# Layer normalisation with its gain and shift applied behind the transposition, in a two-layer decoder trunk on one core

## The chip, the cores and the metric

The kernel runs on one core of one Trainium2 chip. Its time is the device time of one execution in microseconds (us); three runs of the kernel before were timed, and their median is the reference point. Beside them one execution was recorded by the hardware profiler. Five engines work in parallel, each with its own queue of instructions: TensorE (PE, matrix products and transpositions, with its weight loads PEld), VectorE (DVE), ScalarE (ACT), GpSimd (POOL) and SyncE (SP), which here issues nearly all transfers (DMA).

## What is computed

Two layers, each a token mixer and a squared-ReLU feed-forward, in float32, with 1024 positions, a model width of 1024 and a feed-forward width of 4096:

```python
for i in range(2):
    y = dilated_attention_mixer(x, ...) if i == 0 else hgrn2_mixer(x, ...)
    x = layer_norm(alpha * x + y, ln_mix_g[i], ln_mix_b[i])
    y = squared_relu_mlp(x, ffn_w_up[i], ffn_w_down[i])
    x = layer_norm(alpha * x + y, ln_ffn_g[i], ln_ffn_b[i])
```

`layer_norm` subtracts the mean of a row, divides by its standard deviation, multiplies by a gain g and adds a shift b, each a vector of 1024. So every normalised x has two uses: it is the left operand of the next products, and it is the residual of the next sum. Call the value ahead of g and b the unit value.

## The kernel before, in words

A float32 product is made of three matmuls: each operand is split in a high part (an ACT copy that rounds) and a low part (a DVE subtraction), and high times high, low times high and high times low are summed in PSUM. `split` (L137 ACT, L138 DVE) does it for weights and intermediate values, `put` (L233 ACT, L234 DVE) for transposed activations.

The rows of x are held as eight tiles z[t] of 128 positions by 1024. The stages follow one another on the time axis: attention; its output projection with the first normalisation (`outproj_ln`, L886); layer 0's feed-forward (`ffn`, L1015), up products and then down products; the HGRN mixer (`hgrn`, L1482); its `outproj_ln`; layer 1's `ffn`, which ends in the output.

**Normalisation.** `ln_math` (L193) takes statistics on DVE (L196, L198), forms (z - mean) * g in one DVE operation over 128x1024 (L199), the reciprocal deviation r from ACT and small DVE operations (L201 to L206), then z * r on ACT (L213) and + b on POOL (L214). Gain and shift are rows that hold for all partitions; they are loaded as broadcasts of 128x1024. The result is stored to DRAM for the later residual (x1d, x3d, x5d). The output's normalisation uses the variant with `store`, in halves on DVE.

**Transposition.** The products need x with the width on the partitions. `z_tr` (L216) has PE transpose a tile in eight 128x128 pieces (L223) into two PSUM banks of tag "pt" (there are two such banks). In the feed-forward's end `ln_tr` (L236) puts high and low straight from PSUM (the tiles f0n). Ahead of the up products the class `Fast` (L248) prepares a fast matrix scheme with seven products of halves in place of eight: it needs the quarters 11, 21, 22 and the combinations T1 to T4. For the four tiles of the half that comes first, `add` (L271) keeps raw copies (ACT, L291 and L292); for the other half it forms T1 to T4 from PSUM and the copies, with DVE (L298, L301) and POOL (L299, L303) subtracting, after one ACT copy (L297).

**Where the transpositions stand.** In `outproj_ln` four tiles are transposed between the last projections (L994 on), and four are handed to the up products as `late` work, one item for each step with two empty steps ahead of each (L1009 to L1011). In the up products `in_order` (L107, used at L1373) pins PE, DVE and SP to the written order; ACT and POOL are ordered by the framework's scheduler.

**The down products** work through i = 1, 6, 7, 5, 4, 2, each 16 steps of 12 matmuls, and then i = 3 in three passes of 16 steps (6, 3 and 3 matmuls). The steps' loads (`load_down`, L1181 on) run 8 steps ahead, their splits 2 or 4 steps ahead (L45 to L47). Nothing pins their order: L1392 opens `in_order(())`, so the scheduler orders every engine. After each step `after(n)` (L1303) issues loads of the residual (L1306 at i = 7, L1308 at i = 5) and of gain and shift (L1310), and takes one item of a list `todo`: adding products into the residual (`mix` L1278, `plus` L1281), normalising a tile (`norm_of` L1291) and, in layer 0, storing it (L1296) and transposing it (`tr` L1286). In layer 0 tiles 4 to 7 are normalised during i = 2, transposed in the passes, and tiles 0 to 3 are normalised and transposed between the passes; `hgrn` then begins with products of f0n. It takes a `late` list too, one item after each block (L1608), which layer 0's `ffn` returns empty.

Tiles of 128x1024 come from one pool of 50 slots (L90); scratch of 128x512 comes from pool wp with 3 buffers for each of the tags "p" and "pts", which d3s and dT3 (the split operands of i = 3, L1220 on) and the transpositions share.

Of the kernel before, what the change touches and what calls it, by code (L numbers as in the profile page):

```python
# [16 lines left out]
P = 128  # L17
# [45 lines left out]
def trunk_kernel(  # L63
# [15 lines left out]
    w_down: bass.AP,  # L79
    cos_t: bass.AP,  # L80
# [53 lines left out]
    nc.gpsimd.memset(one, 1.0)  # L134

# [57 lines left out]
    def ln_math(z, gB, bB, store=None):  # L193
# [5 lines left out]
        nc.vector.scalar_tensor_tensor(z, z, mv[:, 0:1], gB, op0=ALU.subtract, op1=ALU.mult)  # L199
        w = small([P, 4], "lnw")  # L200
# [6 lines left out]
        if store is not None:  # L207
            for i in range(2):
                c = slice(i * 512, i * 512 + 512)
                nc.vector.scalar_tensor_tensor(z[:, c], z[:, c], w[:, 3:4], bB[:, c], op0=ALU.mult, op1=ALU.add)  # L210
                nc.sync.dma_start(store[:, c], z[:, c])
            return
        act(z, z, AF.Copy, scale=w[:, 3:4])  # L213
        nc.gpsimd.tensor_add(z, z, bB)  # L214
# [21 lines left out]
    def ln_tr(t, z, xs):  # L236
        x_ = xs[t // 4]
        c = slice((t % 4) * P, (t % 4) * P + P)
        for j, pt in enumerate(z_tr(z)):
            put(x_.hi[2 * j:2 * j + 2], x_.lo[2 * j:2 * j + 2], pt, c)  # L240

    class Fast:  # L248


        def __init__(self, name):
            self.name, self.parts, self.raw, self.seen = name, {}, {}, []
# [18 lines left out]
        def add(self, t, z):  # L271
# [3 lines left out]
            v, g = nc.vector, nc.gpsimd  # L275
# [5 lines left out]
            def put_(n, src, eng=None):  # L281
                put(*self.tiles(n), src, c, eng)

            if half == 0:
                put_("11", p0)
                put_("21", p1)
            else:
                put_("22", p1)
            if first:
                a, b = ("11", "21") if half == 0 else ("12", "22")  # L290
                act(self.keep(a, t), p0, AF.Copy)  # L291
                act(self.keep(b, t), p1, AF.Copy)  # L292
                return
            t1, t2, t3, t4 = (scratch(n) for n in (1, 2, 3, 4))
            if half == 1:
                w12 = scratch(0)
                act(w12, p0, AF.Copy)  # L297
                v.tensor_sub(t3, p1, w12)  # L298
                g.tensor_sub(t1, w12, self.keep("11", t))  # L299
                put_("T3", t3)  # L300
                v.tensor_sub(t2, p1, t1)  # L301
                put_("T1", t1)
                g.tensor_sub(t4, self.keep("21", t), t2)  # L303
            else:
                b22 = self.keep("22", t)
                v.tensor_sub(t1, self.keep("12", t), p0)
                g.tensor_sub(t3, b22, self.keep("12", t))
                g.tensor_sub(t2, b22, t1)
                put_("T1", t1)
                v.tensor_sub(t4, p1, t2)  # L310
# [11 lines left out]
    def attention(pre, hc):  # L322
# [124 lines left out]
        def constants():  # L447
            nc.sync.dma_start(cosT, cos_t)
            nc.sync.dma_start(sinT, sin_t)
            nc.sync.dma_start(mask, masks)  # L450

# [434 lines left out]
    def outproj_ln(pr, oN, fill, resid, gB_ap, bB_ap, keep):  # L886
# [84 lines left out]
        gB = bcast_rows(gB_ap, "gB")  # L971
        bB = bcast_rows(bB_ap, "bB")
        second(NK)
        xn = Fast(name + "f")
# [4 lines left out]
        def fin(t, dms=(0, 1)):  # L979
# [10 lines left out]
            if 1 in dms:  # L990
                ln_math(z[t], gB, bB)
# [23 lines left out]
    def ffn(li, xf, late, res, gB_ap, bB_ap, last, pre=None):  # L1015
# [261 lines left out]

        def mix(t, c, other):  # L1278
# [7 lines left out]
        def tr(t):  # L1286
            if xn[t // 4] is None:
                xn[t // 4] = new_xT(t // 4, f"f{li}n")
            ln_tr(t, z[t], xn)

        def norm_of(t):  # L1291
            if last:
                ln_math(z[t], norm["g"], norm["b"], out[t * P:(t + 1) * P, :])
                return
            ln_math(z[t], norm["g"], norm["b"])
            nc.sync.dma_start(x3d[t * P:(t + 1) * P, :], z[t])  # L1296
# [454 lines left out]
```

## Time and profile before

| | us |
|---|---|
| three runs: median (lowest to highest) | 2857.04 (2854.59 to 2858.03) |
| the profiled execution | 2856.82 |
| its span, first to last instruction | 2854.6 |
| PE busy in the span | 2789.4 |
| DVE busy | 2053.8 |
| ACT busy | 1448.4 |
| POOL busy | 122.6 |

On the span's time axis layer 0's up products begin at about 1107, its down products run from 1432 to 1755 (i = 7 from 1519, i = 5 from 1562, the three passes from 1696), HGRN follows, layer 1's up products begin at about 2215 and its down products at 2538.

A line of a group reads: line of the code, engine, operation, what is written <- what is read, its shape, how many (x), then busy time in all and the mean in ns of one, then the idle time of the engine ahead of them and what ended it. A line of the waits reads: engine, what it was about to do, <- what it waited for: total us, times, longest. A row of the timeline: start, length, engine, line, operation, and in brackets the idle time ahead and its releaser.

### The profile page before, as it was taken

How to read it: one execution, taken by the hardware profiler on the slowest of the kernel's cores; microseconds unless marked ns; L12 is line 12 of the kernel's file. 1: busy time of each engine (PE TensorE's matmuls, PEld its weight loads, DVE VectorE, ACT ScalarE, POOL GpSimd, SP SyncE). 2: the span in 40 equal slices, each digit the busy share in tenths (PEclk: the TensorE clock that was granted, in tenths of full speed). 3: DMA queues.
4: the chain of work that ended last, by engine and by line, in shares of the span. 5: the costliest groups of instructions: out<-in, count | busy, mean ns of one | idle time of the engine just before them, and what ended most of it. 6: DMA issues, size and time to landing. Idle time of an engine off the chain costs nothing.

```text
span 2854.6 us, 39893 instructions
## 1 busy us (share of the span) xinstructions
PE 2789.4 (98%) x14152; PEld 2235.3 (78%) x14152; DVE 2053.8 (72%) x3830; ACT 1448.4 (51%) x3105; POOL 122.6 (4%) x67
## 2 busy tenths in 40 slices
PE   8999999999999989999999999999999999999998
PEld 6777777777777767888878887778787788878887
DVE  7768777776887767786686875555667787678677
ACT  5555555655555555544454444554553645454433
POOL 0000000000000003000000011111102200000000
PEclk9999999999999999999999999999999999999999
DMA  7766665666667523464584843101131455475654
GB/s 291 249 201 193 190 197 171 215 206 204 198 198 222 154 77 133 156 220 156 173 303 126 275 142 104 38 30 60 51 120 71 159 202 174 155 268 189 223 176 132
DMA packets 204935, 485.25 MB, mean 170 GB/s; under 512 B 29376, under 2 KB 43712, under 8 KB 204736
## 3 DMA queue, kind: packets, MB, share of 16 engines
q1 hardware_dynamic: 204736, 482.72, 51.3%
q8 instruction: 111, 1.82, 0.3%
q14 instruction: 88, 0.72, 0.1%
HBM read 362.82 MB, written 94.24 MB: 160 GB/s over the span
## 4 chain that ended last, share of the span: by engine, by line
PE 90%; DVE 4%; ACT 2%; DMA 1%; issue 1%; POOL 0%; SPq 0%; DVEq 0%; POOLq 0%; ACTq 0%
PE pmm L666 8%; PE pmm L668 8%; PE pmm L667 8%; PE pup L1114 7%; PE pup L1112 7%; PE pup L1113 7%; PE pdy L1264 4%; PE pdy L1260 4%; PE pdy L1263 4%; PE pmm L171 3%; PE s L500 3%; PE pdx L1263 3%; PE pdx L1264 3%; PE pdx L1260 3%; PE pmm L173 3%; PE pmm L172 3%
## 5 line engine op out<-in xcount | busy, mean ns | idle before, releaser
L666 PE MATMUL pmm<-xh,H 128*128 128x512 f32 x1008 | 407.7, 404 | 12.0 <-ACT H L432 8.5
L668 PE MATMUL pmm<-xh,H 128*128 128x512 f32 x1008 | 396.4, 393 | 0.0
L667 PE MATMUL pmm<-xl,H 128*128 128x512 f32 x1008 | 396.1, 393 | 0.0
L666 PEld LDWEIGHTS pmm<-xh,H 128*128 128x128 f32 x1008 | 191.2, 190 | 52.3 <-ACT H L432 8.5
L668 PEld LDWEIGHTS pmm<-xh,H 128*128 128x128 f32 x1008 | 190.4, 189 | 41.9 <-DVE H L440 0.3
L667 PEld LDWEIGHTS pmm<-xl,H 128*128 128x128 f32 x1008 | 191.1, 190 | 36.9
L514 ACT ACTIVATE p<-p,stats 128x128 f32<-128x128 f32 (+1 forms) x384 | 168.3, 441 | 92.6 <-DVE stats L511 92.2
L1263 PE MATMUL pdy<-dT,dS 128*128 128x512 f32 x512 | 199.2, 389 | 0.0
L1260 PE MATMUL pdy<-dT,dS 128*128 128x512 f32 x512 | 199.2, 389 | 0.0
L1264 PE MATMUL pdy<-dT,dS 128*128 128x512 f32 x512 | 199.2, 389 | 0.0
L511 DVE CUSTOM_DVE_ANT_0 p<-s,mask 128x128 f32<-128x128 f32 (+1 forms) x384 | 113.2, 347 | 68.4 <-PE s L500 58.8
L137 ACT ACTIVATE dS<-dr 128x512 fp32r<-128x512 f32 x192 | 119.5, 622 | 73.3 <-PE pdy L1264 36.6
L171 PE MATMUL pmm<-f0nh,wh 128*128 128x512 f32 x384 | 153.1, 399 | 0.0
L173 PE MATMUL pmm<-f0nh,wl 128*128 128x512 f32 x384 | 149.8, 390 | 0.0
L172 PE MATMUL pmm<-f0nl,wh 128*128 128x512 f32 x384 | 149.6, 390 | 0.0
L138 DVE TENSOR_TENSOR dS<-dr,dS 128x512 fp32r<-128x512 f32 x192 | 135.1, 703 | 16.5 <-ACT dS L137 16.5
L214 POOL TENSOR_TENSOR z<-z,bB 128x1024 f32<-128x1024 f32 x24 | 58.5, 2442 | 1687.8 <-ACT z L213 1678.3
L527 ACT ACTIVATE pts<-ppt 128x256 f32<-128x256 f32 (+1 forms) x192 | 85.3, 474 | 62.7 <-PE ppt L524 60.5
L137 ACT ACTIVATE dT<-hold 128x512 fp32r<-128x512 f32 x128 | 80.0, 625 | 69.5 <-DVE hold L1239 28.8
L1073 ACT ACTIVATE H<-wc 128x512 fp32r<-128x512 f32 x128 | 77.2, 625 | 74.6 <-DVE wc L1066 43.9
L1263 PEld LDWEIGHTS pdy<-dT,dS 128*128 128x128 f32 x512 | 96.1, 188 | 20.0
L1264 PEld LDWEIGHTS pdy<-dT,dS 128*128 128x128 f32 x512 | 96.1, 188 | 20.0
(395 smaller groups left out, 6927.9 us busy)
## 6 DMA issues: line engine op xcount, KB each, us to landing
xh<-xtd SPq DMA_DIRECT2D x110, 512.0 KB
xl<-xtd SPq DMA_DIRECT2D x110, 512.0 KB
dr<-hd SPq DMA_DIRECT2D x192, 256.0 KB
dr<-in_w_down_dram SPq DMA_DIRECT2D x128, 256.0 KB
rot<-e SPq DMA_DIRECT2D x192, 128.0 KB
wa<-in_w_up_dram SPq DMA_DIRECT2D x48, 512.0 KB
wb<-in_w_attn_dram SPq DMA_DIRECT2D x36, 512.0 KB
wa<-in_w_attn_dram SPq DMA_DIRECT2D x33, 512.0 KB
```

Source lines behind the costliest of these rows:

```text
L171: nc.tensor.matmul(o, wh[:, k], xs.h(k), start=k == 0, stop=False)
L172: nc.tensor.matmul(o, wh[:, k], xs.l(k), start=False, stop=False)
L173: nc.tensor.matmul(o, wl[:, k], xs.h(k), start=False, stop=k == NK - 1)
L666: nc.tensor.matmul(o, wh, hi[k // 2][:, c], start=begin and k == 0, stop=False, skip_group_check=True)
L667: nc.tensor.matmul(o, wh, lo[k // 2][:, c], start=False, stop=False, skip_group_check=True)
L668: nc.tensor.matmul(o, wl, hi[k // 2][:, c], start=False, stop=end and k == 3, skip_group_check=True)
L1112: nc.tensor.matmul(o, wh, xf.h(b, k), start=begin and k == 0, stop=False, skip_group_check=True)
L1113: nc.tensor.matmul(o, wh, xf.l(b, k), start=False, stop=False, skip_group_check=True)
L1114: nc.tensor.matmul(o, wl, xf.h(b, k), start=False, stop=end and k == 3, skip_group_check=True)
L1260: nc.tensor.matmul(o[q], h, T_[:, L], start=begin, stop=False, skip_group_check=True)
L1263: nc.tensor.matmul(o[q], h, T_[:, R], start=False, stop=False, skip_group_check=True)
L1264: nc.tensor.matmul(o[q], l, T_[:, L], start=False, stop=end, skip_group_check=True)
```

## The change

The three inner normalisations (both mixers', layer 0's feed-forward) leave the unit value in z: ACT computes z * r - mean * r in one pass (`ln_unit`), and L199 and POOL's L214 are gone for them. Gain and shift come in a new small input `lncol`, one value for each partition, normalisation and block of 128 columns, loaded once. After the transposition a new helper `gained` reads a PSUM bank in four pieces of 128x128 with ACT, times the gain and plus the shift as operands per partition, into SBUF; high and low parts and the combinations T1 to T4 are then taken from that SBUF tile. In `Fast` the kept copies are now `gained` tiles, and what POOL subtracted DVE subtracts.

The residual is now read back as a unit value. In the down products of both layers each residual tile is multiplied by the gain and added to the shift on DVE (`gain`, `bias`), one operation a step from the `todo` list, with the two broadcasts rg and rb loaded at i = 7, and the residual's loads are issued at step 4 of i = 7 (before: 8) and step 2 of i = 5 (before: 8). Layer 0's output x3d still holds the full value: `final` multiplies and adds on DVE and stores, as items of the `late` list for `hgrn`. The output's normalisation is as before, in `ln_last`. `outproj_ln` no longer loads gain and shift. All matmuls and transpositions remain.

```diff
-    def ln_math(z, gB, bB, store=None):
+    def ln_scale(z):
...
-        nc.vector.scalar_tensor_tensor(z, z, mv[:, 0:1], gB, op0=ALU.subtract, op1=ALU.mult)
...
-        act(z, z, AF.Copy, scale=w[:, 3:4])
-        nc.gpsimd.tensor_add(z, z, bB)
+    def ln_unit(z):
+        mv = ln_scale(z)
+        w = ln_rsqrt(mv)
+        nc.vector.tensor_scalar(w[:, 4:5], mv[:, 0:1], w[:, 3:4], -1.0, op0=ALU.mult, op1=ALU.mult)
+        act(z, z, AF.Identity, scale=w[:, 3:4], bias=w[:, 4:5])
...
+    def gained(pt, j, col, dst):
+        for i in range(4):
+            k = j * 4 + i
+            c = slice(i * P, i * P + P)
+            act(dst[:, c], pt[:, c], AF.Identity, scale=lc[:, col, 0, k:k + 1], bias=lc[:, col, 1, k:k + 1])
+        return dst
...
         for j, pt in enumerate(z_tr(z)):
-            put(x_.hi[2 * j:2 * j + 2], x_.lo[2 * j:2 * j + 2], pt, c)
+            raw = gained(pt, j, col, wp.tile([P, 512], F32, name="lnr", tag="p" if j else "pts"))
+            put(x_.hi[2 * j:2 * j + 2], x_.lo[2 * j:2 * j + 2], raw, c)
...
-                act(self.keep(a, t), p0, AF.Copy)
-                act(self.keep(b, t), p1, AF.Copy)
+                r0 = gained(p0, 0, self.col, self.keep(a, t))
+                r1 = gained(p1, 1, self.col, self.keep(b, t))
...
+            r0, r1 = gained(p0, 0, self.col, scratch(0)), gained(p1, 1, self.col, scratch(5))
             t1, t2, t3, t4 = (scratch(n) for n in (1, 2, 3, 4))
             if half == 1:
-                w12 = scratch(0)
-                act(w12, p0, AF.Copy)
-                v.tensor_sub(t3, p1, w12)
-                g.tensor_sub(t1, w12, self.keep("11", t))
+                put_("22", r1)
+                v.tensor_sub(t3, r1, r0)
+                v.tensor_sub(t1, r0, self.keep("11", t))
                 put_("T3", t3)
-                v.tensor_sub(t2, p1, t1)
+                v.tensor_sub(t2, r1, t1)
                 put_("T1", t1)
-                g.tensor_sub(t4, self.keep("21", t), t2)
+                v.tensor_sub(t4, self.keep("21", t), t2)
...
+        def gain(t):
+            v.tensor_mul(z[t], z[t], norm["rg"])
+        def bias(t):
+            v.tensor_add(z[t], z[t], norm["rb"])
+        def scaled(q0):
+            return [lambda t=t, f=f: f(t) for t in range(q0, q0 + 4) for f in (gain, bias)]
+        def final(t):
+            v.tensor_mul(z[t], z[t], norm["g"])
+            v.tensor_add(z[t], z[t], norm["b"])
+            nc.sync.dma_start(x3d[t * P:(t + 1) * P, :], z[t])
...
-            ln_math(z[t], norm["g"], norm["b"])
-            nc.sync.dma_start(x3d[t * P:(t + 1) * P, :], z[t])
+            ln_unit(z[t])
...
+            if j == 4 and i == 7:
+                residual(4)
+                norm["rg"] = bcast_rows(ln_mix_g[li], "rg")
+                norm["rb"] = bcast_rows(ln_mix_b[li], "rb")
             if j == 8 and i == 7:
-                residual(4)
-            if j == 8 and i == 5:
+                todo.extend(scaled(4))
+            if j == 2 and i == 5:
                 residual(0)
+            if j == 6 and i == 5:
+                todo.extend(scaled(0))
...
-        return xn, []
+        return xn, [] if last else [lambda t=t: final(t) for t in (4, 5, 6, 7, 0, 1, 2, 3)]
```

More of the change, by code (lines that the diff above doesn't have):

```diff
@@ L134, in trunk_kernel @@
     nc.gpsimd.memset(one, 1.0)
+    lc = cp.tile([P, 4, 2, NK], F32, name="lncol")
     def split(raw, hi, lo):
@@ L198, in ln_math, with ln_rsqrt @@
         nc.vector.bn_aggr(mv, st)
[L199 to L200 removed]
+        return mv
+    def ln_rsqrt(mv):
+        w = small([P, 5], "lnw")
         act(w[:, 0:1], mv[:, 1:2], AF.Ln, bias=eps_ln)
@@ L883, in pre, with outproj_ln @@
                 self.split_k(k, 0)
-    def outproj_ln(pr, oN, fill, resid, gB_ap, bB_ap, keep):
+    def outproj_ln(pr, oN, fill, resid, keep):
         a = {}
@@ L1012, in outproj_ln, with ffn @@
         return xn, late
-    def ffn(li, xf, late, res, gB_ap, bB_ap, last, pre=None):
+    def ffn(li, xf, late, res, last, pre=None):
         hd = hds[li]
@@ L1729, in _arrays @@
         "w_down": i["ffn_w_down"].reshape(2, NFF, P, D),
+        "lncol": np.stack([np.stack([i[f"ln_{n}_{w}"][l].reshape(NK, P) for w in "gb"])
+                           for l in range(2) for n in ("mix", "ffn")]).transpose(3, 0, 1, 2),
     }
```

73 lines of the change are left out of this document (38 added, 35 removed).

## The prediction

> **What bounds the kernel now.** I read the page's head and chain first, then a table of busy times by stretch, then TensorE's waits in the stretches that the change reaches.
>
> ```profile
> span 2854.6 us, 39893 instructions
> PE 2789.4 (98%) x14152; PEld 2235.3 (78%) x14152; DVE 2053.8 (72%) x3830; ACT 1448.4 (51%) x3105; POOL 122.6 (4%) x67
> PE 90%; DVE 4%; ACT 2%; DMA 1%; issue 1%; POOL 0%; SPq 0%; DVEq 0%; POOLq 0%; ACTq 0%
> ```
>
> TensorE (PE) is the bound: it stands still for 65 us in 2854.6. The change removes no matmul, so it moves the time only by what it does to those 65 us. That VectorE (DVE) is at 72% and ScalarE (ACT) at 51% decides nothing; the stretches do. The columns are the stretch, its length, busy time of PE, weight load, DVE, ACT and POOL, granted clock, DMA share, GB/s.
>
> ```profile
> 1126.00:1170.00 44.00, 42.09 (x195) 33.15 (x194) 34.99 (x66) 31.95 (x77) 11.29 (x8) 1.00 0.39 139
> 2240.00:2285.00 45.00, 43.12 (x196) 33.91 (x195) 33.00 (x62) 30.26 (x72) 8.57 (x6) 1.00 0.42 147
> 1519.00:1541.00 22.00, 22.00 (x99) 18.23 (x98) 18.16 (x30) 9.65 (x18) 0.00 (x0) 1.00 0.62 203
> 1541.00:1562.00 21.00, 21.00 (x95) 17.38 (x94) 6.79 (x11) 8.99 (x17) 0.00 (x0) 1.00 0.32 101
> 1562.00:1584.00 22.00, 22.00 (x99) 18.23 (x98) 21.41 (x36) 10.74 (x19) 0.00 (x0) 1.00 0.71 237
> 1584.00:1606.00 22.00, 22.00 (x99) 18.23 (x98) 13.42 (x22) 7.75 (x14) 0.00 (x0) 1.00 0.93 313
> 1696.00:1766.00 70.00, 62.36 (x292) 49.70 (x291) 49.86 (x107) 37.22 (x88) 10.35 (x5) 0.98 0.29 92
> 1730.00:1735.00 5.00, 3.52 (x21) 2.48 (x20) 1.34 (x4) 1.69 (x5) 5.00 (x3) 1.00 0.26 105
> 1735.00:1740.00 5.00, 1.54 (x11) 0.88 (x9) 4.48 (x10) 2.90 (x10) 0.15 (x1) 1.00 1.05 284
> 1740.00:1745.00 5.00, 4.88 (x17) 3.89 (x18) 3.52 (x11) 3.35 (x9) 0.00 (x0) 0.66 0.94 345
> ```
>
> The change touches four kinds of place: the start of each layer's up products, where the mixer's tiles are transposed (rows one and two: PE loses 1.9 us in each); the down products of i=7 and i=5 (PE full); and the end of layer 0's feed-forward, where the last down product runs in three passes between the transpositions (1696 to 1766: PE loses 7.6 us, two thirds of it between 1730 and 1740). In that last stretch:
>
> ```profile
> PE lnpt L223 <- POOL z L214: 3.2, 3, 1.5
> PE pdx L1260 <- ACT d3s L137: 2.3, 1, 2.3
> PE lnpt L223 <- DVE f0nl L234: 1.5, 3, 0.7
> PE pdx L1260 <- ACT dT L137: 0.7, 2, 0.5
> ```
>
> Behind these waits comes a cold clock (the timeline; its columns are start, length, engine, line):
>
> ```profile
> 1728.04 0.39 PE L1263 MATMUL pdx<-dT,d3s 128*128 128x512 f32 x1
> 1728.26 0.39 PE L1264 MATMUL pdx<-dT,d3s 128*128 128x512 f32 x1
> ...
> 1741.04 0.62 PE L1264 MATMUL pdx<-dT,d3s 128*128 128x512 f32 x1
> ...
> 1744.45 0.48 PE L1263 MATMUL pdx<-dT,d3s 128*128 128x512 f32 x1
> ```
>
> Matmuls start 0.227 us apart at full clock (1728); the eight from 1741.04 on, in the row with clock 0.66, take 3.41 us instead of 1.82. So this stretch loses 7.6 + 1.6 = 9.2 us now.
>
> **Price of one scaled copy.** The trace has no ACT copy of 128x128 out of PSUM with two operands per partition. The nearest rows (mean ns stands behind the bar):
>
> ```profile
> L527 ACT ACTIVATE pts<-ppt 128x512 f32<-128x512 f32 x88 | 50.1, 589 | 18.1 <-PE ppt L524 16.8 <-PE o L539 0.4
> L527 ACT ACTIVATE pts<-ppt 128x256 f32<-128x256 f32 x104 | 36.1, 376 | 44.6 <-PE ppt L524 43.7 <-PE o L539 0.8
> L1567 ACT ACTIVATE oN<-opt,hg 128x512 f32<-128x512 f32 x16 | 10.1, 686 | 8.3 <-PE opt L1566 8.3
> L1602 ACT ACTIVATE ze<-pmm 128x512 f32<-128x512 f32 x16 | 9.5, 595 | 58.2 <-PE pmm L173 58.2
> L233 ACT ACTIVATE afT1h<-fs 128x256 fp32r<-128x256 f32 x8 | 3.1, 409 | 0.0
> 1151.88 0.71 ACT L233 ACTIVATE afT3h<-fs 128x256 fp32r<-128x256 f32 x2
> ```
>
> From L527, 256 columns more cost 213 ns; so 128 columns cost 376 - 106 = 270 with no such operand. One operand costs 686 - 595 = 91. Two give 270 + 182 = 452 ns alone. Two in a row take 0.71 us where one takes 0.409, so a second one adds 0.30: successors overlap by 0.10, and a scaled copy in a row costs **0.35**. From below: 0.30 less 106 for half the columns is 0.20, if the operands hide in the overlap. From above: 0.30 + 0.18 = 0.48, if the overlap that the plain copies show leaves both operands outside. I take 0.35: ACT works these copies in rows of four. A bank is then 1.4 us, a tile 2.8 us.
>
> *A rule against the change:* the Trainium skill, "ScalarE: Activation LUTs", Rules for kernel authors, sends additions and multiplications to VectorE; "What ACT_TABLE_LOAD costs" there gives 186 ns plus 0.833 per column and about 93 for each operand per partition, 479 ns here, an estimate. The rows agree on the operand (91); by its overlap of 93 a copy would be 0.39 and the sum some 2 us more.
>
> **The parts.** The other rows:
>
> ```profile
> L199 DVE SCALAR_TENSOR_TENSOR z<-z,lnmv,gB 128x1024 f32<-128x1024 f32 x32 | 48.5, 1517 | 0.5
> L473 DVE TENSOR_TENSOR rot<-rot,sinT 128x1024 f32<-128x1024 f32 x48 | 58.4, 1217 | 16.2 <-DMA rot<-e 16.2
> L214 POOL TENSOR_TENSOR z<-z,bB 128x1024 f32<-128x1024 f32 x24 | 58.5, 2442 | 1687.8 <-ACT z L213 1678.3 <-issue 5.4 <-ACT lnw L202 4.1
> L298 DVE TENSOR_TENSOR fs<-lnpt,fs 128x512 f32<-128x512 f32 x8 | 5.4, 677 | 0.0
> L297 ACT ACTIVATE fs<-lnpt 128x512 f32<-128x512 f32 x8 | 4.7, 593 | 0.4 <-PE lnpt L223 0.4
> L234 DVE TENSOR_TENSOR afT3l<-fs,afT3h 128x256 fp32r<-128x256 f32 x8 | 5.6, 732 | 0.8 <-ACT afT3h L233 0.8
> L234 DVE TENSOR_TENSOR afT1l<-fs,afT1h 128x256 fp32r<-128x256 f32 x8 | 3.1, 411 | 0.0
> ```
>
> 1. *Normalisation itself* (24 tiles): 24 x 1.517 of DVE and 24 x 2.442 of POOL go, a DVE operation of one column (0.2) comes. POOL's part stood on the path between normalisation and transposition: the 3.2 us above. At the two output projections the transpositions come up to 0.4 us earlier: nothing to 0.4 won, I take nothing, since TensorE runs other products until then.
>
> 2. *Residual in the down products* (both layers): per half, eight DVE operations of 1.217 = 9.7 us, one in each step. In i=7 DVE goes from 6.79 to 16.5 of 21 us; in i=5 from 34.8 to 44.5 of 44 (rows 1562 and 1584). That half microsecond too much hides behind the split's lead of two steps (24 matmuls, 5.4 us) and the emptier product after it. Zero; without that cover 0.5 to 1 per layer. The residual's loads start 4 to 6 steps sooner, out of the stretch with a DMA share of 0.93, and two broadcasts of 128x1024 are added where the share is 0.62 (row 1519): zero. The two broadcasts of outproj go.
>
> 3. *Start of the up products* (each layer). Four tiles of the second half need all combinations. ACT per tile: + 8 x 0.35 - 0.6 (L297) = +2.2; four give +8.8, and ACT goes from 31.95 to 40.8 of 44 (first-half tiles, kept copies replaced, mostly lie before). DVE takes over two POOL subtractions per tile (+2 x 0.68) but its own lows were held beside POOL (732 against 411 ns, x2 per tile): net +0.7, from 35.0 to 38. At 93% in-order ACT makes PE wait where a high half of H or a bank stands behind four copies: I charge one such bank, 1.4, and 0.6 for a transposition behind it: **+2 per layer, +4**. Bounds: -0.5 (the POOL holds go, copies at 0.20) to +4 each (copies at 0.48: ACT at 44.9 of 44).
>
> *A rule for the change:* the Trainium skill, "SBUF — State Buffer", SBUF: two separate sides, calls the port pair of VectorE and GpSimd an exclusive lock for a whole instruction. The 732 against 411 agrees. By that rule alone the up starts would come out faster, by at most the 1.9 us that PE loses in each; that case is part of the faster rival.
>
> ```profile
> 1731.97 1.09 PE L223 MATMUL lnpt<-ident,z 128*128 128x128 f32 x8 [1.28 <-POOL z L214]
> 1731.94 2.68 SPq L1296 DMA_DIRECT2D x3d<-z  x2
> 1734.71 1.47 SPq L1181 DMA_DIRECT2D d<-hd  x2
> 1740.12 0.50 PE L1260 MATMUL pdx<-dT,d3s 128*128 128x512 f32 x1 [2.26 <-ACT d3s L137]
> ```
>
> 4. *End of layer 0's feed-forward.* The queues in the built order:
>  Pass 0: the output's gain and bias for tiles 4, 5 and 6 (two DVE operations, 2.43 a tile), and the stores, now stand ahead of lows that steps 5 and 6 of that pass need. A step is six matmuls, 1.36 us, so each of the first two costs up to 2.43 - 1.36 = 1.1, and the copies of tile 4 ahead of a high part of step 6 some 0.8: **3.0**.
>  Pass 1: tiles 0, 7 and 1, six banks, evacuate in one row on ACT: 24 x 0.35 + 12 high halves x 0.30 = 12.0 us. In it PE has 24 transpositions (0.11 each, from the eight of 1731.97, behind which the next matmul starts 0.85 us later) and 12 matmuls (2.7) = 5.3: **6.7** lost. This is a stretch of transpositions as the one before 1740, so I keep its 1.6 of cold clock.
>  Pass 2: tile 2's eight copies and four highs (4.0) and then a high and a low of 0.42 and 0.45 stand ahead of the pass's first matmul, against 18 matmuls of the next stage (4.1): 0.8; and one more tile's gain and bias (2.43) ahead of a low: **3.2**.
>  Sum 3.0 + 6.7 + 1.6 + 3.2 = 14.5 against 9.2 now: **+5.3**. Bounds: copies at 0.20 make pass 1 3.1 and pass 2 2.4, together 10.1 (+1); at 0.48, 9.8 and 4.2, 18.6 (+9).
>
> 5. *SP's queue.* Two stores that waited for POOL are issued at 1731.94, and only behind them the down weights at 1734.71 whose late arrival is the wait of 2.3 at 1740.12. In the new order one store, behind its bias on DVE, stands there: that load may come 3 us sooner. The 2.3 are then given back, but the copies of pass 1 are already late on ACT by more: counted within pass 1.
>
> Places where the mixer-1 stage and layer 1's down products end (only the output's normalisation, unchanged there) keep their time; half a microsecond for reordered matmuls at the start of layer 0's second stage brings the sum to 4 + 5.3 + 0.5 = **+10**. The profiled execution took 2856.8 us, 2.2 outside its span, and the three runs' median is 2857.0: **2867**.
>
> **Rivals.**
> - *Faster*: POOL and SP bound the end of the feed-forward and ACT has room. The 3.2 go, the 2.3 go with the earlier load, and the cold clock's 1.6 with them; the rest stays, and the up starts win nothing: 2857 - 7 = 2850 (2846 if they win all of 3.8). Decides: copies in a row at about 0.2 us and finals placed behind the lows. For it: 37.2 of 70 us busy on ACT there. Against: the built order has the finals ahead.
> - *Nothing*: new stalls equal old ones; copies near 0.25, up starts unharmed: +1 to +5, 2858 to 2861.
> - *Worse clock*: the row 1740 shows 0.66 after a stretch of transpositions. If the same happens in both up starts and in pass 2, two or three times 1.6 or more come on top: 2870 to 2874.
> - *Slots*: the residual's four tiles come six steps earlier and hold four of 50 slots; if prefetched down weights then start late, PE idles in i=7 and i=5 where it is full now. Loads two steps (5.4 us) late, one in each of the two halves and layers, that the split's lead covers only in part: some 3 us in four places on top of the sum, about 2880.
>
> **How the numbers follow.** Forecast 2863 to 2870: 0.45. Faster 0.19. Nothing 0.2. Clock 0.11. Slots 0.05. The likeliest gives 2867; the range from 2850 to 2874 leaves out the slots, half of the faster rival's tail and little else. 0.2% of the median is 5.7 us, about what a measurement tells from no change: faster 0.18, same 0.22, slower 0.6.
>
> **What would show it.** Mean of the 128x128 copies (452 alone; spacing 0.35). PE's waits at pdx and lnpt between 1696 and 1766: no POOL, instead highs and lows of dT and d3s and the new scaled tiles, 13 us together; DVE's timeline with gain and bias ahead of a d3s low; one clock row near 0.66. The rows 1126 and 2240 should lose 3 to 4 us each, with ACT above 40; i=7 and i=5 should stay full. It is wrong if PE's loss from 1696 to 1766 falls below 7 us, if the copies cost under 0.25, or if PE loses time in a place that none of these steps names.

## The result and the profile after

The changed kernel takes 2875.1 us (median of six runs, 2872.5 to 2876.6); the kernel before, run beside it, 2857.3 (2854.6 to 2860.5). The ratio is 1.006, its 95% interval 1.0049 to 1.0071: 18 us slower. The forecast was 10 us slower, 2867, with a range that ended at 2874.

The head of the page after:

```profile
span 2872.2 us, 40020 instructions
PE 2796.7 (97%) x14152; PEld 2240.6 (78%) x14152; DVE 2066.1 (72%) x3894; ACT 1503.6 (52%) x3273; POOL 41.7 (1%) x27
PE 88%; DVE 5%; ACT 3%; issue 2%; DMA 2%; SPq 0%; POOL 0%; DVEq 0%; POOLq 0%; ACTq 0%
```

GpSimd has lost 81 us and ScalarE gained 55, and the sums over the span say no more than that. Where the 17.6 us of span lie is read from the first starts of groups that both kernels have. In the answer about one tile, each row ends its times with "first to last start"; ahead of that stand the shortest, median and longest ns. Before:

```profile
L1112 PE MATMUL pup<-af11h,H x64: 388/389/496, 1118.3 to 1414.1; 128*128 128x512 f32 x64
...
L1260 PE MATMUL pdx<-dT,dS x256: 388/389/503, 1431.7 to 2714.6; 128*128 128x512 f32 x128
...
L1260 PE MATMUL pdx<-dT,d3s x128: 389/389/628, 1695.0 to 2845.2; 128*128 128x512 f32 x128
...
L1508 PE MATMUL as<-qe,ls x128: 274/275/580, 1803.2 to 2120.4; 128*128 128x128 f32 x128
```

And after:

```profile
L1129 PE MATMUL pup<-af11h,H x64: 389/389/757, 1117.5 to 1418.6; 128*128 128x512 f32 x64
...
L1277 PE MATMUL pdx<-dT,dS x256: 388/389/498, 1436.2 to 2732.7; 128*128 128x512 f32 x128
...
L1277 PE MATMUL pdx<-dT,d3s x128: 387/389/776, 1699.6 to 2863.3; 128*128 128x512 f32 x128
...
L1544 PE MATMUL as<-qe,ls x128: 275/275/582, 1815.9 to 2133.9; 128*128 128x128 f32 x128
```

The first row is where layer 0's up products begin, the second its down products, the third its three passes, the fourth HGRN's recurrence. Differences of neighbouring starts give the length of each stage; layer 1's up products are taken from the first start of hf11h to the last of hf22h. By these starts layer 0's up products begin at 1118.3 in the kernel before and layer 1's at 2225.8, not at about 1107 and 2215 as written above. The forecast of +5.8 is step 4's 5.3 and the half microsecond behind it.

| stage | before | after | difference | forecast |
|---|---|---|---|---|
| start to the first up product, layer 0 | 1118.3 | 1117.5 | -0.8 | 0 |
| up products, layer 0 | 313.4 | 318.7 | **+5.3** | +2 |
| down products up to the passes, layer 0 | 263.3 | 263.4 | 0.1 | 0 |
| passes and HGRN's first products | 108.2 | 116.3 | **+8.1** | +5.8 |
| HGRN's recurrence | 317.2 | 318.0 | +0.8 | 0 |
| output projection, mixer 1 | 105.4 | 103.4 | **-2.0** | 0 |
| up products, layer 1 | 312.4 | 319.0 | **+6.6** | +2 |
| down products, layer 1, and tail | 316.4 | 315.9 | -0.5 | 0 |

The stretches that answer to those of before, moved by the stage's start (same columns):

```profile
1126.00:1174.00 48.00, 41.70 (x186) 32.95 (x185) 34.77 (x73) 41.47 (x105) 0.00 (x0) 0.96 0.35 125
1134.00:1142.00 8.00, 4.97 (x16) 3.87 (x17) 6.40 (x15) 7.08 (x19) 0.00 (x0) 0.79 0.23 90
2246.00:2294.00 48.00, 41.69 (x186) 32.90 (x185) 34.78 (x73) 41.20 (x105) 0.00 (x0) 0.96 0.36 125
1523.50:1545.50 22.00, 22.00 (x99) 18.22 (x98) 15.38 (x25) 8.74 (x16) 0.00 (x0) 1.00 0.72 235
1545.50:1566.50 21.00, 21.00 (x94) 17.39 (x93) 18.11 (x24) 9.73 (x17) 0.00 (x0) 1.00 0.35 106
1588.50:1610.50 22.00, 22.00 (x99) 18.21 (x98) 22.00 (x34) 6.80 (x12) 0.00 (x0) 1.00 0.92 301
1700.60:1779.00 78.40, 67.50 (x294) 52.81 (x292) 58.04 (x117) 54.60 (x141) 0.96 (x1) 0.91 0.39 125
```

Both up starts now lose 6.3 us of TensorE, where they lost 1.9, with ScalarE busy for 41 of 48 us, and a granted clock of 0.79 in eight of them. The down products stay full: TensorE is busy for all of the 22 us in which VectorE is too (1588.5). The residual's scaling is free. In the passes 10.9 us are lost, where 7.6 were, at a clock of 0.91.

TensorE's waits after, in layer 0's up start (those of layer 1 have the same three rows):

```profile
PE pup L1129 <- ACT H L1090: 2.8, 2, 1.7
PE lnpt L243 <- ACT fs L233: 2.1, 1, 2.1
PE pup L1129 <- ACT upa L1134: 1.4, 1, 1.4
```

All of them are waits for ScalarE. In the passes GpSimd is gone from the list, and ScalarE stands there instead:

```profile
PE pdx L1277 <- ACT d3s L139: 4.0, 2, 2.7
PE lnpt L243 <- ACT lnr L233: 3.4, 3, 1.4
PE pdx L1277 <- ACT dT L139: 1.6, 1, 1.6
PE lnpt L243 <- ACT z L217: 1.0, 1, 1.0
PE pdx L1281 <- DVE d3s L140: 0.8, 1, 0.8
```

How one wait is followed by a second and then by a low clock is seen in the timeline of layer 0's up start. TensorE's rows with idle time ahead of them:

```profile
1135.35 0.66 PE L243 MATMUL lnpt<-ident,z 128*128 128x128 f32 x4 [2.08 <-ACT fs L233]
1137.69 0.76 PE L1129 MATMUL pup<-af11h,H 128*128 128x512 f32 x1 [1.69 <-ACT H L1090]
1159.84 0.50 PE L1129 MATMUL pup<-af21h,H 128*128 128x512 f32 x1 [1.41 <-ACT upa L1134]
1171.66 0.50 PE L1129 MATMUL pup<-afT2h,H 128*128 128x512 f32 x1 [1.09 <-ACT H L1090]
```

and ScalarE's at the first of them:

```profile
1126.48 2.90 ACT L233 ACTIVATE fs<-lnpt,lncol 128x128 f32<-128x128 f32 x8
...
1132.87 0.46 ACT L233 ACTIVATE fs<-lnpt,lncol 128x128 f32<-128x128 f32 x1 [0.82 <-PE lnpt L243]
1133.23 0.41 ACT L253 ACTIVATE afT1h<-fs 128x256 fp32r<-128x256 f32 x1
1133.54 0.45 ACT L233 ACTIVATE fs<-lnpt,lncol 128x128 f32<-128x128 f32 x1
...
1134.83 0.46 ACT L233 ACTIVATE fs<-lnpt,lncol 128x128 f32<-128x128 f32 x1
...
1136.48 1.16 ACT L1090 ACTIVATE H<-wa 128x512 fp32r<-128x512 f32 x2
```

The scheduler has put twelve transpositions behind one another, three banks where two exist. The third waits until the first is empty, and that takes four pieces, with the previous tile's highs in between: from 1132.87 to 1135.29. Then H's highs begin only at 1136.48, behind six pieces and five highs, and TensorE waits for them until 1137.69. From 1132.2 to 1137.7 it has run nothing but transpositions, and its next eight matmuls start about 0.43 us apart:

```profile
1138.24 0.63 PE L1130 MATMUL pup<-af11l,H 128*128 128x512 f32 x1
1138.67 0.63 PE L1129 MATMUL pup<-af21h,H 128*128 128x512 f32 x1
```

In the kernel before the same twelve take from 1133.1 to 1136.0, and the matmuls behind them start at the full pace:

```profile
1133.09 1.03 PE L223 MATMUL lnpt<-ident,z 128*128 128x128 f32 x8
1134.46 0.63 PE L223 MATMUL lnpt<-ident,z 128*128 128x128 f32 x4 [0.34 <-ACT fs L297]
1135.99 0.50 PE L1112 MATMUL pup<-af11h,H 128*128 128x512 f32 x1 [0.90 <-ACT H L1073]
```

### The profile page after: what moved, and what is told of

It is laid out like the page before. It is cut to its first block, busy times and chain, and to the rows that moved or that the text cites. A ratio compares the mean times of both kernels' runs of the same rounds, so it can differ in the third digit from the quotient of the medians.

```text
span 2872.2 us, 40020 instructions
## 1 busy us (share of the span) xinstructions
PE 2796.7 (97%) x14152; PEld 2240.6 (78%) x14152; DVE 2066.1 (72%) x3894; ACT 1503.6 (52%) x3273; POOL 41.7 (1%) x27
## 4 chain that ended last, share of the span: by engine, by line
PE 88%; DVE 5%; ACT 3%; issue 2%; DMA 2%; SPq 0%; POOL 0%; DVEq 0%; POOLq 0%; ACTq 0%
PE pmm L685 7%; PE pmm L687 7%; PE pmm L686 7%; PE pup L1129 7%; PE pup L1131 7%; PE pup L1130 7%; PE pdy L1280 4%; PE pdy L1277 4%; PE pdy L1281 4%; PE pdx L1281 3%; PE pdx L1280 3%; PE pdx L1277 3%; PE s L519 3%; PE pmm L173 3%; PE pmm L174 2%; PE pmm L175 2%
## 5 line engine op out<-in xcount | busy, mean ns | idle before, releaser
L685 PE MATMUL pmm<-xh,H 128*128 128x512 f32 x1008 | 407.1, 404 | 12.1 <-ACT H L450 8.8
L1277 PEld LDWEIGHTS pdy<-dT,dS 128*128 128x128 f32 x512 | 96.1, 188 | 20.1
L1281 PEld LDWEIGHTS pdy<-dT,dS 128*128 128x128 f32 x512 | 96.1, 188 | 19.9
L1280 PEld LDWEIGHTS pdy<-dT,dS 128*128 128x128 f32 x512 | 96.1, 188 | 19.8
```

Source lines behind the costliest of these rows:

```text
L685: nc.tensor.matmul(o, wh, hi[k // 2][:, c], start=begin and k == 0, stop=False, skip_group_check=True)
L1277: nc.tensor.matmul(o[q], h, T_[:, L], start=begin, stop=False, skip_group_check=True)
L1280: nc.tensor.matmul(o[q], h, T_[:, R], start=False, stop=False, skip_group_check=True)
L1281: nc.tensor.matmul(o[q], l, T_[:, L], start=False, stop=end, skip_group_check=True)
```

## The experiments

Each kernel was run beside the kernel before on the same chip. Ratios are to those runs (medians 2858.3 for the first four, 2859.8, 2856.7 and 2858.6 for the next groups). The last columns are the stages of the table above from each one's own profile: both up products, and the passes.

| kernel | median us | ratio (95%) | up 0 | up 1 | passes |
|---|---|---|---|---|---|
| before | 2857.3 | 1 | 313.4 | 312.4 | 108.2 |
| after | 2875.1 | 1.0060 (1.0049 to 1.0071) | 318.7 | 319.0 | 116.3 |
| e1 mixers as before | 2864.6 | 1.0020 (1.0011 to 1.0030) | 313.0 | 312.0 | 115.9 |
| e2 feed-forward as before | 2869.5 | 1.0037 (1.0024 to 1.0050) | 319.6 | 318.0 | 108.8 |
| e3 one plain copy | 2853.4 | 0.9986 (0.9976 to 0.9995) | 313.1 | 312.3 | 107.2 |
| e4 pieces on VectorE | 2866.5 | 1.0032 (1.0020 to 1.0043) | 318.4 | 317.6 | 111.0 |
| e5 half on VectorE | 2868.4 | 1.0030 (1.0017 to 1.0044) | 319.5 | 317.3 | 109.7 |
| e6 GpSimd subtractions | 2869.9 | 1.0039 (1.0026 to 1.0052) | 318.1 | 315.5 | 114.8 |
| e7 before, shift on VectorE | 2847.2 | 0.9969 (0.9957 to 0.9981) | 312.8 | 311.9 | 104.2 |
| e8 no finals | 2873.3 | 1.0050 (1.0035 to 1.0065) | 320.1 | 318.7 | 112.9 |
| e9 ScalarE's order, later part | 2874.9 | 1.0057 (1.0040 to 1.0074) | 319.9 | 317.9 | 116.4 |
| e10 TensorE's order | 2887.0 | 1.0106 (1.0091 to 1.0122) | 328.3 | 322.7 | 114.7 |
| e11 ScalarE's order | 2916.2 | 1.0205 (1.0188 to 1.0222) | 340.9 | 339.1 | 115.9 |
| e12 before, TensorE's order | 2889.3 | 1.0113 (1.0098 to 1.0128) | 329.8 | 329.2 | 108.9 |
| e13 bank first | 2882.6 | 1.0086 (1.0071 to 1.0101) | 321.7 | 322.3 | 118.7 |
| e14 bank first, VectorE | 2866.1 | 1.0024 (1.0015 to 1.0033) | 315.9 | 315.3 | 115.5 |
| e15 e7, subtractions on VectorE | 2853.5 | 0.9984 (0.9974 to 0.9993) | 316.1 | 315.4 | 104.6 |

A stage length comes from one execution, and the low clock differs between places with the same waits: after, e8 and e9 show the same four waits in every up start, but in layer 0's 8, 12 and 13 slow matmuls (0.43 us apart in place of 0.227), so that it lasts 318.7, 320.1 and 319.9 us. A length can thus differ by 1.4 us or more with the waits unchanged; where two kernels lie closer than that, TensorE's waits are compared as well.

**Does each place pay by itself?** e1 gives both mixers back what they had before and leaves only layer 0's feed-forward changed (the residual's earlier loads stay); e2 is its complement.

```diff
 # e1: Fast.add, outproj_ln and the residual of before
-                ln_unit(z[t])
+                ln_math(z[t], gB, bB)
 # e2: norm_of, ln_tr and the stores of before
-            ln_unit(z[t])
+            ln_math(z[t], norm["g"], norm["b"])
```

> Both mixers' normalisations, the combinations T1 to T4 and the residual are as in the kernel before; only layer 0's feed-forward end is as after. Theory A (each place pays by itself: the up starts pay for ScalarE's copies, the feed-forward's end for its own queue): the two up starts' losses of about 6 us each go, and the two output projections' gains of 0.8 and 2.0 us with them: 2875 - 12 + 2.8 = 2866. Rival B (the places are coupled, because buffers and queues carry a delay of one into the next): not additive, within 3 us of 2875 or of 2857.

> Complement: layer 0's feed-forward ends as in the kernel before, the mixers and the residual in the down products are as after. Theory A: 2875 less the 8 to 9 us that lie between the first matmul of the three passes and HGRN's recurrence = 2866 to 2867, with up starts that still lose 6.3 us each and the residual's gain and bias at zero. Rival B: far from that. If the residual's scaling on VectorE costs something, i = 7 and i = 5 show idle TensorE here too.

Measured: 6.4 and 11.2 us above their runs of before, together 17.6, against 17.8 for the whole change. In e1 the up products have the length of before and the passes that of after; in e2 it is the other way round. Theory A holds, rival B is out: the places are not coupled. e1 lies 1.4 us below its figure and e2 3 us above; the execution that was profiled of e2 was its fastest (2865.7). e2's profile has the residual's scaling too, with no difference in the down products (263.4).

**Is it the number of copies?** e3 makes one plain copy of the four pieces of a bank, without gain and shift.

```diff
-        for i in range(4):
-            k = j * 4 + i
-            c = slice(i * P, i * P + P)
-            act(dst[:, c], pt[:, c], AF.Identity, scale=lc[...], bias=lc[...])
+        act(dst, pt, AF.Copy)
```

> The four scaled copies of a bank are one plain copy of 128x512 (gain and shift are left out of the transposed x); order, buffers and VectorE's share of the subtractions stay. A tile costs ScalarE about 2 x 0.5 = 1.0 us in place of 2.8. Theory A (ScalarE's time per bank): the up starts lose 2 to 3 us each in place of 6.3, no cold clock there, the passes 4 us less: 2859 to 2863. Rival C (it is the longer chain bank - copy - split and VectorE's additional subtractions, whatever ScalarE takes): 2870 or more.

Measured: 2853.4, 4.9 below its runs of before and, by the two ratios, some 21 below after; better than theory A had it, and rival C is out. The waits of its up start, the long one of 2.1 shrunk to 0.3:

```profile
PE pup L1126 <- ACT H L1087: 1.9, 2, 1.5
PE lnpt L240 <- ACT fs L230: 0.3, 1, 0.3
```

Everything else of the change is in this kernel: the splits from SBUF, the subtractions on VectorE, the residual's scaling, the finals, 16 transpositions in a row in the built order. So with one copy per bank all the rest of the change wins 5 us, and the four scaled pieces in its place lose 21. Two things go at once here, the number of copies and their two operands. By the prediction's lower bound a plain piece in a row would take 0.20 us, four of them 0.8 against 0.6 for one copy and 1.4 for the scaled four; by that estimate the operands weigh more than the number. No run separates them. The built order differs too: twelve transpositions stood in the longest row of after.

**Is it ScalarE?** e4 puts the pieces on VectorE, e5 half of them.

```diff
-            act(dst[:, c], pt[:, c], AF.Identity, scale=lc[...], bias=lc[...])
+            nc.vector.tensor_scalar(dst[:, c], pt[:, c], lc[...], lc[...], op0=ALU.mult, op1=ALU.add)
```

> The same four pieces of each bank on VectorE (multiply and add with two operands per partition) in place of ScalarE. Theory A: H's high halves are on time again; VectorE takes 8 pieces of about 0.3 us a tile, in the up starts from 46 to about 58 of 72 us, and in the passes it is already at 60 of 70: up starts about +2 to 3 each, passes no better or worse than after: 2862 to 2870. Rival C: 2873 or more, since the chain from bank to split is as long as in after.

> Of a bank's four scaled pieces two are on ScalarE and two on VectorE, side by side. Theory A, in the form that the first four runs leave (what counts is how long a bank's copies hold a queue and the bank itself, 4 x 0.35 on ScalarE as well as on VectorE; one copy of 0.6 costs nothing): a bank is free after about 0.75 us, so most of the loss goes: 2859 to 2863. If it is the total work on the two engines that counts, whichever carries it, there is no gain over the kernel with all pieces on VectorE: 2865 to 2868.

Measured: the passes win 5.3 and 6.6 us against after, the up starts 0.3 to 1.7 (e5's first is 0.8 longer). In e4's up start the same wait is there under another name:

```profile
PE lnpt L243 <- DVE fs L233: 2.7, 1, 2.7
PE pup L1131 <- DVE H L1098: 1.8, 1, 1.8
PE pup L1129 <- ACT H L1090: 1.2, 1, 1.2
```

e4's 2866.5 us lies where theory A had it, but by luck: the passes, which were to gain nothing, are 5.3 us shorter, and the up products, which were to lose 2 to 3 us against before, lose 5. Rival C is out. In the passes ScalarE was the late engine. In the up starts TensorE waits as long as in after (5.8 and 6.7 us in place of 6.3). e5's first expectation failed and its second holds: two engines side by side are no better than one (1.0030 against 1.0032), and TensorE's wait at that place is 2.0 again, now for VectorE. The reading that fits is that a bank is free only when both engines have come to it, each with its own queue of the previous tile's parts ahead; that was not tried by itself.

**The other additions.** e6 returns two subtractions per tile to GpSimd, e8 leaves the finals' arithmetic out.

```diff
 # e6
-                v.tensor_sub(t1, r0, self.keep("11", t))
+                nc.gpsimd.tensor_sub(t1, r0, self.keep("11", t))
 # e8
-            v.tensor_mul(z[t], z[t], norm["g"])
-            v.tensor_add(z[t], z[t], norm["b"])
```

> As after, but two of the subtractions for T1 and T4 are back on GpSimd (1.4 us each, the copies T1 to T4 otherwise as after). Theory A: VectorE has room there, so 2873 to 2879, the same or a little slower through the longer chain. Rival D (the subtractions moved to VectorE are what makes the up starts late): 2 us or more back in each, 2871 or less.

> As after, but x3d holds the unit value: the multiplication by gain and the addition of shift on VectorE between the passes are left out (the later residual lacks them). By step 4 of the prediction they cost 2 x 1.1 in the first pass and 2.4 in the third: 2870 to 2871. If ScalarE's copies alone set the passes: 2874 to 2876. Up starts unchanged in both.

e6 wins about a third of the loss back (1.0039 in place of 1.0060, though the intervals overlap slightly). Its time lies where rival D had it, its stages only in part: 0.6 and 3.5 us less in the up products, 1.5 in the passes. TensorE's waits in each up start fall by 1.3, from 6.3 to 5.0; the rest is the clock, with eight slow matmuls in layer 0's and none in layer 1's. So beside the pieces the subtractions seem to cost VectorE something, against theory A; beside one copy (e3) no loss shows. e8's passes are 3.4 us shorter than after's, where step 4 had 4.6; in its time, 2873.3 where 2870 to 2871 was expected, that is 1.0050 in place of 1.0060, inside the intervals. Layer 0's up products are 1.4 us longer than after's by the clock alone, with the same waits. e8 is not simply the finals' price: leaving them out also changed the built order of other engines.

**Is it the order?** Layer 0's and layer 1's late transpositions fall into the first 16 up products, which nothing pins; the pinned order begins behind them (`if n == 2 * NAHEAD`). e9 added ScalarE to the pinned engines and so changed only what lies behind.

```diff
 # e9
-        order = in_order((mybir.EngineType.PE, mybir.EngineType.DVE, mybir.EngineType.SP, ))
+        order = in_order((mybir.EngineType.PE, mybir.EngineType.DVE, mybir.EngineType.SP, mybir.EngineType.Activation))
 # e10 and e12 (PE, on after and on before), e11 (Activation, on after)
+        early = in_order((mybir.EngineType.PE,))
+        early.__enter__()
         for n in range(len(seq)):
             if n == 2 * NAHEAD:
+                early.__exit__()
```

> As after, but in the up products ScalarE too follows the written order (only its queue changes, 516 rows of difference), in which a tile's eight pieces stand in one row ahead of its splits instead of being mixed with the splits of the tile before. Rival E (the scheduler's mixing delays the bank's release and so makes the wait of 2.1 and the cold clock): 2 us or more back in each up start, 2871 or less. Theory A (the load itself): 2872 to 2880, since the high halves of H then stand behind whole rows of pieces.

> As after, but in the first 16 up products TensorE follows the written order: one tile's eight transpositions, then 36 matmuls, four times, where the scheduler had put 12 transpositions in one row (8, 24 matmuls, 12, 26, 3, ...). Theory F (the loss in the up starts comes from transpositions placed too close together for the time that a bank's copies now take, so that the third bank waits, the row of transpositions alone lasts over 5 us, and the clock falls): the waits of 2.1 and 1.7 and the cold clock go, each up start loses 2 to 3 in place of 8: 10 us less than after. Theory A (ScalarE's load, 91% there, whatever the order): within 3 us of after.

> As after, but ScalarE follows the written order in those first 16 products (e9 pinned it only behind them, so that rival E was not put to the test there). TensorE's order becomes 8 transpositions, 24 matmuls, 8, 24, 8, 48, 8 with it. Theory F: no third bank in one row, so a good part comes back: 4 to 8 us less than after. Theory A: within 3 us of after.

> Control: the kernel before with TensorE pinned as in e10. Its up starts lose 1.9 us each, 0.3 and 0.9 of it at the same place, so 0 to 2 us less in both together: within 3 us of before. Were it as much faster as e10 is against after, the order and not the change would be what counts.

e9 shows the same four waits to 0.02 us, and tells nothing on rival E. e10 and e11 missed theory F's figures by far, and so did the control: the written order costs the kernel before 16.4 and 16.8 us in the up starts, with new waits for a bank that ScalarE has to empty (12.0 us at upa), and with ScalarE's written order (e11) the up products last 20 to 22 us longer than after's. But e10 against e12 says something: with eight transpositions and then 36 matmuls, four times, the changed kernel's up products are no longer than before's (328.3 and 322.7 against 329.8 and 329.2), and TensorE waits no longer in them (11.4 and 11.5 us against 12.0 and 12.1); no wait for a transposition's bank is left. The price of the pieces is not fixed. It depends on the slack that the order leaves around them.

**Bank or engine?** e13 and e14 empty a bank with one plain copy first and then scale in SBUF.

```diff
+        act(dst, pt, AF.Copy)
         for i in range(4):
...
-            act(dst[:, c], pt[:, c], AF.Identity, scale=lc[...], bias=lc[...])
+            act(dst[:, c], dst[:, c], AF.Identity, scale=lc[...], bias=lc[...])    # e13; e14: nc.vector.tensor_scalar
```

> As after, but a bank is first copied whole by one plain ScalarE copy (0.6 us), and the four scaled pieces then work in place in SBUF, on ScalarE: 1.0 us more load a tile than after, the bank free in 0.6 in place of 1.4. If the bank's hold counts: the wait of 2.1 and the cold clock (1.6) go in each up start, 2875 - 7 or lower. If ScalarE's load counts: each up start loses 2 to 5 us more than after, the passes too: 2880 to 2890.

> The same with the four pieces on VectorE, from SBUF to SBUF: ScalarE as in the kernel with one plain copy, VectorE with the load of the kernel with its pieces. If the bank's hold counts: up starts near 313 us, as with one plain copy. If the load on the engine that also makes the low halves counts: near 318, as in the kernel with pieces on VectorE out of PSUM.

The waits of e13's up start:

```profile
PE pup L1130 <- ACT H L1091: 6.4, 3, 4.5
PE pup L1132 <- DVE H L1099: 1.2, 1, 1.2
PE lnpt L244 <- ACT fs L230: 0.8, 1, 0.8
PE pup L1130 <- ACT upa L1135: 0.4, 1, 0.4
```

The wait for the bank falls from 2.1 to 0.8, and the wait for H's highs rises from 2.8 to 6.4: each up start is 3 us longer than after's. That is the expectation for ScalarE's load; freeing the bank gives nothing while ScalarE carries more. In e14, with the bank free (0.4) and the load on VectorE, the up products are 2.8 and 3.0 above e3's where after's are 5.6 and 6.7: half of the loss is left. Against e4, with its held banks (318.4 and 317.6), e14 is 2.4 us shorter in each. This fits that ScalarE's load is the larger cause and that freeing the bank pays once the load is on VectorE; it is not shown cleanly, because a piece also takes VectorE less time from SBUF (341 against 402 ns) and the built order has changed in e13 and e14 (16 transpositions in one row). Of the remainder, eight matmuls at the low clock are 1.7 us in layer 0, where TensorE idles only 2.9 us; layer 1 has none and waits 3.9 us. In the passes e14 does not gain: 115.5 us against e4's 111.0, with waits of 1.2, 0.7 and 2.2 us for VectorE's lows of d3s and 2.7 for a tile's normalisation.

**A faster kernel.** e7 keeps the kernel before and takes GpSimd out of the normalisation; e15 also moves the four subtractions.

```diff
 # e7
-        act(z, z, AF.Copy, scale=w[:, 3:4])
-        nc.gpsimd.tensor_add(z, z, bB)
+        nc.vector.scalar_tensor_tensor(z, z, w[:, 3:4], bB, op0=ALU.mult, op1=ALU.add)
 # e15, on top
-                g.tensor_sub(t1, w12, self.keep("11", t))
+                v.tensor_sub(t1, w12, self.keep("11", t))
```

> The kernel before, with one VectorE operation (z times r plus the shift, 1.5 us) in place of ScalarE's z times r (1.15) and GpSimd's addition (2.44). The normalisation's chain is 2 us shorter, GpSimd and its hold on VectorE are gone, no scaled pieces come. If GpSimd on the chain is what the change does well (3.2 us of waits in the passes, 0.8 and 2.0 at the output projections): 4 to 6 us less than before. If VectorE becomes the bound between the passes (50 of 70 us now, 6 more): 0 to 2 less.

> The fastest so far (the kernel before with one VectorE operation for z times r plus the shift), with GpSimd's subtractions for T1 to T4 on VectorE as in after. If those subtractions cost nothing by themselves, the up starts stay at 312 to 313 us and the time within 3 us of 2847; if they are part of the loss, 315 or more each.

e7 takes 2847.2 us, 9.5 below its runs of before, more than the 4 to 6 expected, and by the two ratios some 26 below after: it beats both. The passes are 4.0 us shorter, mixer 1's output projection 2.0 (103.4). The operation costs VectorE less than I had taken for it, and so does the one ahead of it. In the kernel before that one took 1517 ns in the mean: five of its 32 took 2.2 to 3.4 us, each beside an operation of GpSimd, and the others 1.27 to 1.29. In e7:

```profile
L199 DVE SCALAR_TENSOR_TENSOR z<-z,lnmv,gB 128x1024 f32<-128x1024 f32 x32 | 40.9, 1279 | 0.4
L213 DVE SCALAR_TENSOR_TENSOR z<-z,lnw,bB 128x1024 f32<-128x1024 f32 x24 | 30.7, 1278 | 0.2
```

e15 gives back about half by the ratios, 0.9984 against 0.9969, though the intervals overlap. Its profiled execution (span 2858.2) is the slowest of its ten, and its stage lengths of 316 contain eight matmuls at the low clock in each up start. But TensorE also waits longer there, 3.9 us in each where e7 has 1.6. So the second expectation fits, and the subtractions, with the order that was built around them, cost some 2 us in each up start. In e3, where they read two SBUF tiles, no such loss shows.

## Why the prediction was wrong, point by point

*Price of a copy*: right. Eight in a row take 2.90 us, so one after another costs 0.35, as forecast; alone 468 against 452.

```profile
L233 ACT ACTIVATE fs<-lnpt,lncol 128x128 f32<-128x128 f32 x64 | 25.2, 468 | 1.6 <-PE lnpt L243 1.6
L254 DVE TENSOR_TENSOR afT3l<-fs,afT3h 128x256 fp32r<-128x256 f32 x8 | 3.1, 417 | 0.0
```

*Step 1*, normalisation: the one gain taken at nothing was worth 2.0 us at mixer 1's output projection (shown in every kernel without GpSimd's addition: 103.1 to 103.4, against 105.4 to 105.5 with it), while the first output projection's 0.8 lies within what that stage differs between executions. The second row above also shows GpSimd's hold gone (732 to 417 ns), as expected.

*Step 2*, residual: right, zero.

*Step 3*, the up starts, is the step that failed. It read the engine and the mechanism rightly (ScalarE at 41 us, H's highs and a bank behind copies) and mis-sized the term: it charged one bank, 1.4, and one transposition, 0.6, where four waits of 2.1, 1.7, 1.4 and 1.1 came, 6.3 in place of 1.9, and the clock with them. Two things were missed. A bank's release was priced at its four pieces, but the scheduler laid the previous tile's highs between them (2.4 us from the first piece to the release). And one stall does not stay one: H's highs were queued behind the same pieces. The upper bound, 4 per layer, was made from busy time, 44.9 of 44, which holds no such chain. The sum also had nothing for a low clock in the up starts. +12 in place of +4 is nearly all of the miss by place. By cause, against the forecast: 4.8 us more waiting in the up starts, 3.3 of low clock there, 3.7 more of it in the passes, and on the other side 2.0 less waiting in the passes and the 2.0 won at mixer 1's output projection.

*The clock* was set aside as a rival with a chance of 0.11; its 2870 to 2874 came nearest. Slow matmuls follow the long stretch in both up starts (1.7 and 1.6 us), and in the passes they take 5.3 us instead of the 1.6 that step 4 kept: 24 of them last 10.7 us, where 0.227 each would be 5.4. What brings the low clock about the runs show only in part (last section).

*Step 4*, the passes: +8.1 against 5.8. The waits by pass are 2.3, 5.1 and 3.5 us, where the step had 3.0, 6.7 and 3.2; so the waiting was put 2 us too high and the clock 3.7 too low. Together they are 16.2 in place of 9.2 before; the last microsecond of the 8.1 was not followed. In pass 0 both waits are for ScalarE (1.6 for a high of dT, 0.7 for a bank), not for lows behind gain and bias; the only wait for a low is the 0.8 above. The copies and the finals do both count: e4, with the copies on VectorE, has passes 5.3 us shorter, and e8, without the finals' arithmetic, 3.4.

*Step 5*, SP's queue: wrong in its sign, without effect. The stores of the finals now wait for VectorE and hold the down weights back:

```profile
1733.91 8.31 SPq L1307 DMA_DIRECT2D x3d<-z  x2
1742.31 1.45 SPq L1198 DMA_DIRECT2D d<-hd  x2
```

Measured from the start of the passes the load is 3.0 us later, not sooner (42.7 against 39.7). It was covered: the matmul that waits longest, 2.7 us, is released by a d3s that ScalarE began at 1753.41, right behind eight pieces and four highs.

*The rivals*: the faster one named the gain rightly, GpSimd off the chain, and e7 has it (4.0 in the passes and 2.0 at the output projection) without the pieces that hid it. Slots did not show.

## What to carry to other kernels

Price a step that empties PSUM banks by the time from the first transposition to the bank's release in the in-order queue of the engine that empties it, with everything that stands between, and not by its busy time; where matmuls and transpositions alternate, ask for the number of banks that one row of transpositions needs. Four small scaled copies in place of one plain copy cost some 21 us here although they moved no more data, and moving them to another engine hardly shortened the waits in the up starts. Where TensorE's stretches without matmuls grow, leave room in the sum for a low clock behind them: here the clock cost 7 us more than the sum had for it. If one engine is too slow on a chain, replace it there (e7: one fused operation in place of two engines) before rearranging the mathematics around it.

## What the runs showed of the hardware

In the up starts of the changed kernel, e8 and e9 a stretch of twelve transpositions and two waits takes 5.45 us (1132.2 to 1137.7 in after), and 7 to 13 matmuls at the low clock follow, 0.43 us apart, in six up starts out of six. In the kernel before, e1 and e7 the same twelve take 2.9 us (1133.1 to 1136.0 in before), and none follows, again in six out of six. The Trainium skill, "TensorE: Matmul & The Clock Gate", Part 4: PE-mode transpose, says that a transposition does not count as busy for the clock in the way that a matmul does; these stretches agree with it.

The length alone does not decide. In e6 a stretch of 4.1 us is followed by eight slow matmuls in layer 0 and by none in layer 1. e10 has 28 of them in its first up start and none in its second, with the same order and the same six waits to 0.1 us. What else decides stays open.

A VectorE piece of 128x128 out of PSUM with two operands per partition takes 402 ns in the mean in e4, against ScalarE's 468 in after, and 341 from SBUF in e14.
